# Transposed inputs and GpSimd-queued weights in the in-projection of a hybrid attention and gating layer, with early maxima by key block and re-laid attention pools

## The chip, the cores and the metric

The kernel runs on one core of a Trainium2 chip. The metric is the device time of one execution in microseconds, lower is better; before and after are compared on the same chip. Of the core's engines, TensorE (PE) multiplies matrices, VectorE (DVE), ScalarE (ACT) and GpSimd (POOL) work on elements, and SyncE (SP) only issues transfers here.

## The reference

One pre-norm layer on 2048 tokens of width 1024, all in float32: an input projection, eight heads of attention with forget gates beside a spatial gating unit, an output projection, a gated feed-forward, and a last norm. What matters here is the projection and attention.

```python
xn = rms_norm(x, mix_norm_g)                       # x / rms(x) * gain
h = xn @ w_in                                      # widths: q 512, k 512, v 512, f 8, z 1024
log_f = log_sigmoid(f_logit + b_f); c = cumsum(log_f)
s = q @ k.T / 8 + c[:, None] - c[None, :]          # per head, causal
attn = softmax(s) @ v
sgu = spatial_gating(gelu(z), ...)
x = x + concat(rms_norm(attn), rms_norm(sgu)) * on_g @ w_out
x = x + (silu(gate) * up) @ w_down                 # [gate, up] = rms_norm(x) * ffn_g @ w_gu
out = rms_norm(x) * fin_g
```

## The kernel before

**Products.** A float32 factor is kept as two halves in the format fp32r, hi = round(a) and lo = a - hi, and a product is three matmuls: hi·hi, hi·lo and lo·hi. `hi_of` (L101) is a cast on ACT, `lo_of` (L106) a subtraction on DVE. `T` takes a tile from a pool; a pool's `bufs` is how many tiles of one name live at a time. The order of each engine's instructions is set by a tile scheduler from the program order and from when tiles come free, so it differs from the order in which the code is written; what must wait waits on semaphores. Nearly all transfers are issued by SP, in the order that the scheduler gave its queue.

**Stage 1, the in-projection,** goes over four chunks of 512 tokens (`for c in range(NCH)`). For a chunk, `x_prep` loads four tiles of 128 tokens (L202), squares and sums them on ACT (L205), takes the power -1/2 on POOL (L148), scales on DVE (L207), transposes on PE against `ident` (L216: 8 of 128x128 a tile) and makes the halves from PSUM with the norm's gain (hi on ACT L220, lo on DVE L221). They are also stored to `XS`, from which z is made later. x_prep is a generator: its steps for chunk c+1 run between the blocks of chunk c. A chunk's blocks of 24 matmuls are: the forget gates' (`pf`, 16 matmuls, L376), q and k (4 head pairs each, L397) and V (4 token tiles, `v_tile`, L343). Accumulators `mm` have four banks. `load_w` brings a weight in four pieces of 128 x 2 x 512 (512 KB) through `rawp`, two buffers (L163), and makes its halves (L101, L106).

**The gates' rows.** `forget_rows(j)` turns chunk j's gate logits into running sums and writes them to `AUG`, two rows a chunk that are added to the scores as two more rows of the contraction; it writes eight rows of 128 at a time (40 transfers in all), and `load_const` fills the rest of AUG from a row of constants.

**Early maxima.** Softmax needs each query's maximum, and for chunk j the heads 0 to `HE[j]` get theirs in stage 1, during chunk j+1: `early_max` loads the head's queries `A` and key chunks `D` (four buffers), and `row_max` runs, for each of four query tiles and each key chunk, one matmul (L275) and one reduction on DVE (L277, on the diagonal L280). `max_split` and `max_rows` (L293, L295) turn the result into a row. `between(n)` runs n of these evaluations in the slot behind each block, n = 3, 6, 6 in chunks 1, 2, 3 (from `EB = 12`), and steps the other generators.

**Stage 2, attention,** frees stage 1's pools and opens its own. For each key block `qk` makes scores (L494, L495, on the diagonal a mask L497 from `idr` and `kmask`), exp on ACT (L499) and halves `Ph`, `Pl`; `pv` follows (L510 to L512). V tiles `V0`… carry columns of ones that POOL writes (L445). z's projection (L542) is woven in from `XS` with weights `wzv` and `wzu`, loaded in chunk 3. Output projection and feed-forward follow.

Of the kernel before, what the change touches and what calls it, by code (L numbers as in the profile page):

```python
# [74 lines left out]
def trunk(ctx: ExitStack, tc: tile.TileContext, x, mix_g, w_in, b_f, ln_g, ln_b, w_st, b_st, on_g, w_out,  # L75
# [80 lines left out]
    def load_w(p, src, tag):  # L156

        wh = T(p, [P, KT, 512], F32R, tag + "h")
        wl = T(p, [P, KT, 512], F32R, tag + "l")
        v = src.rearrange("(k p) n -> p k n", p=P)  # L160
        for i in range(4):
            raw = T(rawp, [P, 2, 512], F32, "raw")
            ld(raw, v[:, 2 * i : 2 * i + 2, :])  # L163
# [12 lines left out]
    ld(mixc, mix_g.rearrange("(k p) -> p k", p=P))  # L176
    def load_const():
# [5 lines left out]
        for h in range(H):  # L183
            ldr(AUG[h, 0:8, :].rearrange("r (o n) -> r o n", n=CH),
                CR[4:5].rearrange("r (o n) -> r o n", o=1).broadcast_to([8, NCH, CH]))
            ldr(AUG[h, 8:10, :].rearrange("r (o n) -> r o n", n=CH),
                CR[32:34].rearrange("r (o n) -> r o n", o=1).broadcast_to([2, NCH, CH]))

    CR = T(dram, [34, CH], F32R, "CR")
    wv = None  # L190

    def x_prep(c, xh, xl):
        xp = p1 if c % 2 else xev
        for i in range(4):
            xh.append(T(xp, [P, 2, CH], F32R, "xh", bufs=4))
            xl.append(T(xp, [P, 2, CH], F32R, "xl", bufs=4))
        xts = {}

        def scaled(tt):
            t = c * 4 + tt  # L200
            xt = T(p1x, [P, D], F32, "xt")
            ld(xt, x[t * P : (t + 1) * P, :])  # L202
# [1 line left out]
            ss = T(p1, [P, 1], F32, "ss")
            nc.scalar.activation(jk, xt, AF.Square, accum_out=ss)  # L205
            r = rsqrt(p1, ss, 1.0 / D, "r1")
            nc.vector.tensor_scalar_mul(xt, xt, r)  # L207
            xts[tt] = xt

        def turned(tt):  # L210
            t, xt = c * 4 + tt, xts[tt]
            o = slice(tt * P, (tt + 1) * P)
            for g in range(2):
                tp = T(ps1, [P, 4, P], F32, "tp")
                for kk in range(4):
                    nc.tensor.transpose(tp[:, kk, :], xt[:, (g * 4 + kk) * P : (g * 4 + kk + 1) * P], ident)  # L216
                for kk in range(4):
                    k = g * 4 + kk
                    h_, l_ = xh[k // 2][:, k % 2, o], xl[k // 2][:, k % 2, o]
                    nc.scalar.activation(h_, tp[:, kk, :], AF.Copy, scale=mixc[:, k : k + 1])  # L220
                    nc.vector.scalar_tensor_tensor(l_, tp[:, kk, :], mixc[:, k : k + 1], f(h_), ALU.mult, ALU.subtract)  # L221
# [999 lines left out]
```

## Time and profile before

| what | us |
|---|---|
| median of 3 executions (2527.21 to 2529.3) | 2529.13 |
| profiled execution | 2529.99 |
| its span | 2528.2 |
| PE busy in it | 2450.9 |
| start to chunk 1's first matmul | 102.5 |
| chunks 1 to 3 | 253.9 |
| last projection matmul to first z matmul | 41.5 |

The profile shows one execution: for each engine the time it was busy, tables of windows and of groups of instructions, and timelines, in which a bracket gives the idle time before an instruction and what released it. A line such as L216 is a line of the kernel before. A PE instruction's shown length is that of its way through the array; the next one starts earlier, so that costs are taken from the distance between starts. The granted clock is PE's, as a share of the full one.

### The profile page before, as it was taken

The numbers are of one execution on the slowest core, as the hardware profiler recorded it, in microseconds if no ns is written. First come the engines' busy times: TensorE is split into PE (matmuls) and PEld (weight loads), VectorE is DVE, ScalarE is ACT, GpSimd is POOL, SyncE is SP. The second block draws the span as 40 slices with busy tenths as digits, with TensorE's granted clock in tenths as the row PEclk, the third lists the DMA queues.
The fourth block names the chain that finished last, engine by engine and source line by source line (L and its number), as shares of the span: only waits on it lengthen the run. The fifth ranks groups of instructions, "written<-read, shape, count | busy, mean of one in ns | idle before, by whom it ended". The sixth has DMA issues, their size and how long they took to land. (4 is left out here: it accounts for less than half of the span.)

```text
span 2528.2 us, 31431 instructions
## 1 busy us (share of the span) xinstructions
PE 2450.9 (97%) x10956; PEld 1962.8 (78%) x10956; DVE 1571.9 (62%) x2636; ACT 1071.2 (42%) x1877; POOL 547.2 (22%) x438
## 2 busy tenths in 40 slices
PE   7999979999999998999999999999999999999998
PEld 5777857787777776887788888878888877888876
DVE  5367464555556657446655555685555586596887
ACT  5333116677776676433433233432332342232333
POOL 0000000000000015112223223233232224454441
PEclk9999989999999998999999999999999999999999
DMA  8654556344333325575432222242322235455354
GB/s 265 207 193 154 183 158 161 96 116 111 97 90 93 111 76 151 172 241 172 158 96 79 84 84 78 83 140 84 97 71 84 84 112 190 174 175 187 133 187 151
DMA packets 348806, 339.89 MB, mean 134 GB/s; under 512 B 54444, under 2 KB 273708, under 8 KB 347624
## 3 DMA queue, kind: packets, MB, share of 16 engines
q1 hardware_dynamic: 348648, 337.88, 43.5%
q8 instruction: 87, 1.43, 0.2%
q14 instruction: 71, 0.58, 0.1%
HBM read 221.74 MB, written 116.72 MB: 134 GB/s over the span
## 5 line engine op out<-in xcount | busy, mean ns | idle before, releaser
L101 ACT CAST wh<-raw 128x512 fp32r<-128x512 f32 (+2 forms) x500 | 309.7, 624 | 809.4 <-PE pp L1163 646.1
L106 DVE TENSOR_TENSOR wl<-raw,wh 128x512 fp32r<-128x512 f32 (+2 forms) x500 | 374.6, 758 | 111.8 <-ACT wh L101 111.4
L106 DVE TENSOR_TENSOR Pl<-Pt,Ph 128x512 fp32r<-128x512 f32 (+1 forms) x320 | 200.8, 633 | 201.5 <-ACT Ph L101 191.4
L894 POOL TENSOR_TENSOR raw<-raw 128x512 f32<-128x512 f32 (+1 forms) x124 | 166.0, 1340 | 549.2 <-DMA raw<-in_w_gu_dram 368.0
L499 ACT ACTIVATE Pt<-st 128x512 f32<-128x512 f32 (+1 forms) x320 | 168.4, 532 | 159.6 <-PE st L495 86.9
L542 PE MATMUL z<-wh,xz 128*128 128x512 f32 x512 | 201.4, 403 | 0.0
L101 ACT CAST Ph<-Pt 128x512 fp32r<-128x512 f32 (+1 forms) x320 | 176.2, 556 | 14.4 <-DVE Pl L106 2.5
L894 DVE TENSOR_TENSOR raw<-raw,raw 128x512 f32<-128x512 f32 (+1 forms) x112 | 133.9, 1197 | 73.9 <-POOL raw L894 69.6
L277 DVE TENSOR_REDUCE mx<-mx_ps 128x1 f32<-128x512 f32 x192 | 128.0, 685 | 32.0 <-PE mx_ps L275 31.0
L275 PE MATMUL mx_ps<-D,A 72*128 72x512 f32 (+5 forms) x320 | 123.6, 409 | 13.3 <-DVE mx L277 5.6
L512 PE MATMUL pv<-Pl,V 128*128 128x512 f32 (+1 forms) x320 | 122.1, 382 | 8.1 <-DVE Pl L106 8.0
L510 PE MATMUL pv<-Ph,V 128*128 128x512 f32 (+1 forms) x320 | 122.8, 384 | 2.4 <-DMA V<-VD 2.0
L494 PE MATMUL st<-A,D 74*128 74x512 f32 (+1 forms) x320 | 122.1, 382 | 0.9 <-ACT Pt L499 0.7
L495 PE MATMUL st<-B,C 128*128 128x512 f32 (+1 forms) x320 | 120.2, 376 | 0.0
L511 PE MATMUL pv<-Ph,V 128*64 128x512 f32 (+1 forms) x320 | 117.4, 367 | 0.0
L542 PEld LDWEIGHTS z<-wh,xz 128*128 128x128 f32 x512 | 96.6, 189 | 18.2
L1163 PE MATMUL pp<-R2h,wh 128*128 128x512 f32 x264 | 105.0, 398 | 5.2 <-ACT u L952 5.2
L1163 PE MATMUL pp<-R3h,wl 128*128 128x512 f32 x264 | 104.1, 394 | 2.6 <-DVE wl L106 2.6
L1163 PE MATMUL pp<-R2h,wl 128*128 128x512 f32 x264 | 104.9, 397 | 0.3 <-DVE wl L106 0.2
L1163 PE MATMUL pp<-R1h,wh 128*128 128x512 f32 x264 | 104.4, 395 | 0.3 <-ACT wh L101 0.3
L1163 PE MATMUL pp<-R3h,wh 128*128 128x512 f32 x264 | 104.6, 396 | 0.0
L1163 PE MATMUL pp<-R5h,wh 128*128 128x512 f32 x264 | 104.5, 396 | 0.0
(311 smaller groups left out, 6250.0 us busy)
## 6 DMA issues: line engine op xcount, KB each, us to landing
raw<-in_w_gu_dram SPq DMA_DIRECT2D x88, 512.0 KB
HD<-hT SPq DMA_DIRECT2D x44, 512.0 KB
xz<-XS SPq DMA_DIRECT2D x32, 512.0 KB
XA<-xa SPq DMA_DIRECT2D x27, 512.0 KB
xa<-XA SPq DMA_DIRECT2D x24, 512.0 KB
raw<-HD SPq DMA_DIRECT2D x24, 512.0 KB
xb<-XA SPq DMA_DIRECT2D x24, 512.0 KB
XA<-xb SPq DMA_DIRECT2D x21, 512.0 KB
```

The costliest lines, as they stand in the source:

```text
L101: nc.scalar.copy(o, i)
L106: eng.tensor_tensor(o, i, f(h), ALU.subtract)
L275: nc.tensor.matmul(pm[:, 0:n], lhs, rhs_of(s, n), start=True, stop=True)
L277: nc.vector.tensor_reduce(mx[:, a, s : s + 1], pm, AX.X, ALU.max)
L494: nc.tensor.matmul(st[:, off:], Dt[:, b * P : (b + 1) * P], A[:, off:], start=True, stop=False)
L495: nc.tensor.matmul(st[:, off:], C[:, b * P : (b + 1) * P], B[:, off:], start=False, stop=kb < 4 * j)
L499: nc.scalar.activation(Pt[:, off:], st[:, off:], AF.Exp)
L510: nc.tensor.matmul(pv[:, off:], V[:, 0:P], Ph[:, off:], start=kb == 0, stop=False)
L512: nc.tensor.matmul(pv[:, off:], V[:, 0:P], Pl[:, off:], start=False, stop=kb == 4 * j + 3)
L542: nc.tensor.matmul(pz, xz[:, a, k, :], w[b][:, k, :], start=n == 0, stop=n == 3 * KT - 1)
L894: (nc.vector if e == "v" else nc.gpsimd).tensor_tensor(o, a, b, op)
L1163: nc.tensor.matmul(pm, a[:, k, :], b[:, k, :], start=on is None and k == 0 and e == 0, stop=k == it.kh - 1 and e == 2, skip_group_check=n ...
```

## The change

**Transposed input.** The host passes x also transposed (`x_t`). Class `Chunk` takes the place of x_prep: it loads x_t in four pieces of 512 KB a chunk and makes halves straight from them. The norm's factor depends on the token, which now lies along the free axis: the four factors' columns are transposed by PE into a row on all partitions (`row`, 4 transposes a chunk of a broadcast column) and x_t is multiplied by it (`rb`) on DVE. Natural tiles of x are still loaded for the squares. In chunk 0 the halves are made without the factor, and V, q, k, the gates and z are multiplied by it at eviction.

**Start.** 13 matmuls on a tile of zeros (`still`) stand first on PE. Pieces of x_t and of wv (in five pieces) alternate on SP; V of chunk 0 is accumulated k by k in four banks at a time (`v_open`, `v_part`, `v_close`).

**Weights.** wq, wk, wzv and wzu are issued by GpSimd. wzu's first two pieces are asked for behind chunk 3's first V tile, its halves made behind the loop. The gate weight has 40 columns in place of 128.

**Maxima and AUG.** AUG is laid out [block and head, row, 128], and a chunk's rows are written by one transfer; the constants are two, from tiles that POOL sets. `early_max` goes key chunk by key chunk over the four query tiles (`one_max`), with loads j+1 ahead and five D buffers; EB by chunk gives 3, 6 and 7 evaluations a slot.

**Attention's pools.** V0 and V1 get a pool of their own (`p2v`), with their ones set early by DVE; the pool of Pt, Ph and Pl, and the PSUM pools of scores and pv are set apart and re-ordered; idr and kmask are made in the start. `v` has two buffers.

```diff
-EB = 12
+EB = [1, 12, 12, 10]
+ND = 5
-    AUG = T(dram, [H, 10, S], F32R, "AUG")
+    AUG = T(dram, [NB * H, 10, P], F32R, "AUG")
+    def weight(p, src, tag, pieces=PC, eng=nc.gpsimd):
...
+            wide = tag == "wv" and n_raw[0] % 4 > 1
+            raw[i] = T(p1x, [P, 2, 512], F32, "xt") if wide else T(rawp, [P, 2, 512], F32, "raw")
+            raw[i] = raw[i][:, 0 : o.stop - o.start]
+            eng.dma_start(raw[i], v[:, o, :])
...
+    class Chunk:
...
+        def halves(self, i, ms=(0, 1)):
+            raw = self.raw[i]
+            if self.c:
+                nc.vector.tensor_tensor(raw, raw, self.rb.rearrange("p (o n) -> p o n", o=1).broadcast_to([P, 2, CH]),
+                                        ALU.mult)
+            for m in ms:
...
+                nc.scalar.activation(h_, raw[:, m], AF.Copy, scale=mixc[:, k : k + 1])
+                nc.vector.scalar_tensor_tensor(l_, raw[:, m], mixc[:, k : k + 1], f(h_), ALU.mult, ALU.subtract)
...
+        def square(self, tt, xt):
             jk = T(p1, [P, D], mybir.dt.bfloat16, "jk", bufs=1)
+            nc.scalar.activation(jk, xt, AF.Square, accum_out=self.ss[:, tt : tt + 1])
             if tt == 3:
+                a = T(p1, [P, 4], F32, "r1a")
+                nc.vector.tensor_scalar(a, self.ss, 1.0 / D, EPS, ALU.mult, ALU.add)
+                nc.gpsimd.tensor_tensor(r1[:, self.c * 4 : self.c * 4 + 4], a, mhalf, ALU.pow)
+        def row(self):
+            tp = T(ps1, [P, 4, P], F32, "tp")
+            for tt in range(4):
+                t = self.c * 4 + tt
+                nc.tensor.transpose(tp[:, tt, :], r1[:, t : t + 1].broadcast_to([P, P]), ident)
+            self.rb = T(p1, [P, CH], F32, "rb", bufs=1) if self.c else T(p1, [P, CH], F32, "D", bufs=ND)
+            nc.scalar.copy(self.rb, tp.rearrange("p a t -> p (a t)"))
...
-        for b in range(4 * j + 4):
-            ldr(AUG[:, 2 * j : 2 * j + 2, b * P : (b + 1) * P], augs[8 * b : 8 * b + 8])
+        n = 8 * (4 * j + 4)
+        ldr(AUG[0:n, 2 * j : 2 * j + 2, :], augs[0:n])
...
+    def early_max(j):
+        jobs = [(h, s) for h in range(HE[j]) for s in range(j + 1)]
...
+        PF = j + 1
+        for n in range(PF):
+            get(n)
+        for n, (h, s) in enumerate(jobs):
+            get(n + PF)
...
             for a in range(4):
+                one_max(ps1, p1, a, j, s, As[h][:, a * P : (a + 1) * P], Ds[n], mx)
+                yield
...
+        if xc.c:
+            hi_of(nc.scalar, v[:, :, 0:DH], pmv)
+            lo_of(nc.vector, v[:, :, DH:P], pmv, v[:, :, 0:DH])
+        else:
+            r = r1[:, tt : tt + 1]
+            nc.scalar.activation(v[:, :, 0:DH], pmv, AF.Copy, scale=r)
...
+    still = T(p1, [P, CH], F32R, "D", bufs=ND)
+    nc.vector.memset(f(still), 0.0)
+    pm = T(ps1, [P, CH], F32, "mx_ps")
+    for _ in range(13):
+        nc.tensor.matmul(pm, still[:, 0:P], still, start=True, stop=True)
+    wv, get_v, halves_v = weight(wvp, w_in[:, 1024:1536], "wv", [slice(0, 1), slice(1, 2)] + PC[1:], nc.sync)
...
+    wq = whole(wgt, w_in[:, 0:512], "w")
+    load_mats()
+    pms = [v_open() for _ in range(4)]
+    for k in range(KT):
+        for tt in range(4):
+            v_part(pms[tt], nxt, tt, [k])
+    nxt.row()
+    for tt in range(4):
+        v_close(pms[tt], nxt, tt)
+    wk = whole(wgt, w_in[:, 512:1024], "w")
...
+                if c == 0:
...
+                    nc.vector.tensor_tensor(qs, pm, xc.rb, ALU.mult)
...
+            if c == NCH - 1 and tt == 0:
+                wzu, get_u, halves_u = weight(wgt, w_in[:, 1544:2056], "w")
+                get_u(0)
+                get_u(1)
...
+    for i in range(4):
+        if i > 1:
+            get_u(i)
+        halves_u(i)
...
+    p2v = pool(st2, "p2v", bufs=1)
     p2c = pool(st2, "p2c", bufs=1)
+    p2h = pool(st2, "p2h", bufs=2)
     p2 = pool(st2, "p2", bufs=2)
+    psv = pool(st2, "psv", bufs=2, side="right", space=PSUM)
+    pst = pool(st2, "pst", bufs=2, space=PSUM)
...
+    with tc.high_priority():
+        for v in vt[:2]:
+            nc.vector.memset(f(v[:, :, DH:P]), 1.0)
```

What the scheduler makes of it, engine by engine; the name left of the arrow is written, those on its right are read, and "x4" stands for four such rows in a chain. PE at the program's start, before: `tp` are the transposed x, `mm` an accumulator of V.

```order
L216 MATMUL tp_277<-ident_63,xt_239 128x128 x4
L216 MATMUL tp_290<-ident_63,xt_239 128x128 x4
L343 MATMUL mm_303<-wvh_259,xh_231 128x512
L343 MATMUL mm_303<-wvl_260,xh_231 128x512
L343 MATMUL mm_303<-wvh_259,xl_232 128x512
```

PE at the start, after: L438 are the matmuls on zeros, L418 those of V, `mm` of four numbers the four tiles' accumulators.

```order
L438 MATMUL mx_ps_242<-D_240 128x512 x13
L418 MATMUL mm_353<-wvh_256,xh_231 128x512
L418 MATMUL mm_354<-wvh_256,xh_231 128x512
L418 MATMUL mm_355<-wvh_256,xh_231 128x512
L418 MATMUL mm_356<-wvh_256,xh_231 128x512
L418 MATMUL mm_353<-wvl_257,xh_231 128x512
```

The transposes are gone, and V's first matmuls alternate between four accumulators. ACT ahead of chunk 0's gate, after: L102 on `wh` are the casts of wq and wk, L260 the squares, L428 V's evictions, L490 the eviction of the gate.

```order
L102 CAST wh_330<-raw_336 128x1024
L260 ACTIVATE jk_319,ss_239<-xl_311 128x1024
L260 ACTIVATE jk_321,ss_239<-xl_313 128x1024
L102 CAST wh_330<-raw_340 128x1024
L102 CAST wh_330<-raw_344 128x1024
L428 ACTIVATE xh_460<-mm_353,r_2_64 128x8x64
L428 ACTIVATE xh_464<-mm_354,r_2_64 128x8x64
L428 ACTIVATE xh_468<-mm_355,r_2_64 128x8x64
L272 COPY D_458<-tp_453 128x512
L428 ACTIVATE xh_472<-mm_356,r_2_64 128x8x64
L102 CAST wh_476<-raw_478 128x1024
```

The same place on ACT before: L101 on `v` are V's evictions, L220 the halves of x.

```order
L101 CAST v_328<-mm_303 128x8x64
L220 ACTIVATE xh_237<-tp_355,mixc_226 128x128
L101 CAST wh_533<-raw_535 128x1024
L220 ACTIVATE xh_237<-tp_355,mixc_226 128x128
L101 CAST wh_533<-raw_539 128x1024
```

V's evictions now stand in a group behind all four casts of wq. PE at the hand-over to attention, before: L275 are the last head's maxima, L293 turns them into a row, L494 and L495 are the first scores.

```order
L275 MATMUL mx_ps_3583<-D_3508,A_3505 128x512
L275 MATMUL mx_ps_3586<-D_3511,A_3505 128x512
L275 MATMUL mx_ps_3589<-D_3514,A_3505 128x512
L293 MATMUL tp_3627<-ident_63,mh_3624 8x128
L494 MATMUL st_3743<-A_3709,D_3704 128x512
L495 MATMUL st_3743<-B_3712,C_3701 128x512
L494 MATMUL st_3768<-A_3709,D_3704 128x384
```

PE at the hand-over, after: L418 is the last V block's end, L354 the same turn, L624 to L627 the first scores.

```order
L418 MATMUL mm_3259<-wvh_256,xh_1680 128x512
L418 MATMUL mm_3259<-wvl_257,xh_1680 128x512
L418 MATMUL mm_3259<-wvh_256,xl_1684 128x512
L354 MATMUL tp_3189<-ident_63,mh_3186 8x128
L624 MATMUL st_3389<-A_3355,D_3350 128x512
L625 MATMUL st_3389<-B_3358,C_3347 128x512
L627 MATMUL st_3389<-kmask_68,idr_67 128x128
L624 MATMUL st_3414<-A_3355,D_3350 128x384
```

The maxima have moved ahead of the last V block, and the scores follow it directly.

More of the change, by code (lines that the diff above doesn't have):

```diff
@@ L74, in trunk @@
 @with_exitstack
[L75 removed]
+def trunk(ctx: ExitStack, tc: tile.TileContext, x, x_t, mix_g, w_in, b_f, ln_g, ln_b, w_st, b_st, on_g, w_out,
           ffn_g, w_gu, w_down, fin_g, c_mat, c_row, out):
@@ L154, in trunk @@
     rawp = pool(wstk, "rawp", bufs=2, side="right")
-    def load_w(p, src, tag):
+    PC = [slice(2 * i, 2 * i + 2) for i in range(4)]
+    n_raw = [0]
+    def weight(p, src, tag, pieces=PC, eng=nc.gpsimd):
         wh = T(p, [P, KT, 512], F32R, tag + "h")
@@ L182, in load_const @@
         ldr(CR, crr)
[L183 to L202, printed above, removed]
-            jk = T(p1, [P, D], mybir.dt.bfloat16, "jk", bufs=1)
[L204 to L221, printed above, removed]
-            if tt == 3:
-                for i in range(4):
-                    ldr(XS[c][:, 0, 2 * i : 2 * i + 2, :], xh[i])
-                    ldr(XS[c][:, 1, 2 * i : 2 * i + 2, :], xl[i])
-        for fn, tt in ((scaled, 0), (scaled, 1), (turned, 0), (scaled, 2), (turned, 1), (scaled, 3), (turned, 2),
-                       (turned, 3)):
-            fn(tt)
@@ new lines, in trunk @@
+    nxt = Chunk(0)
+    still = T(p1, [P, CH], F32R, "D", bufs=ND)
[4 more added lines that the diff above has]
+    wv, get_v, halves_v = weight(wvp, w_in[:, 1024:1536], "wv", [slice(0, 1), slice(1, 2)] + PC[1:], nc.sync)
+    for m in range(2):
+        nxt.get(0, (m,))
+        get_v(m)
+    for i in range(1, 4):
+        nxt.get(i)
+        get_v(i + 1)
+    for m in range(2):
+        nxt.halves(0, (m,))
+        halves_v(m)
@@ new lines, in trunk @@
+    for i in range(1, 4):
+        nxt.halves(i)
+        halves_v(i + 1)
+    wfr = T(p1, [P, KT, H], F32, "fT", bufs=1)
+    ld(wfr, w_in[:, 1536:1544].rearrange("(k p) n -> p k n", p=P))
+    bfc = T(p1, [H, 1], F32, "bfc", bufs=1)
+    ld(bfc, b_f.rearrange("(h o) -> h o", o=1))
+    nat = [nxt.natural(tt) for tt in range(4)]
+    for i in range(4):
+        nxt.square(i, nat[i])
+    wf = T(p1, [P, KT, 40], F32R, "wf", bufs=1)
+    nc.vector.memset(f(wf), 0.0)
+    nc.vector.tensor_copy(wf[:, :, 0:8], wfr)
@@ L422, in trunk @@
         early = early_max(c) if c < NCH - 1 else iter(())
+    for i in range(4):
+        if i > 1:
+            get_u(i)
+        halves_u(i)
     st1.close()
@@ L437, in trunk @@
     wst_l = T(p2z, [P, 8, P], F32R, "wstl", bufs=1)
[L438 to L444 removed]
+    vt = [T(p2v if i < 2 else p2c, [P, 4, 192], F32R, f"V{i}", bufs=1) for i in range(NC_)]
+    with tc.high_priority():
+        for v in vt[:2]:
+            nc.vector.memset(f(v[:, :, DH:P]), 1.0)
+    for v in vt[2:]:
         nc.gpsimd.memset(f(v[:, :, DH:P]), 1.0)
@@ L474, in prep @@
             for a in range(4):
-                yield from row_max(ps2, p2, a, j, A[0:72, a * P : (a + 1) * P],
-                                   lambda s, n: kd[h, s][1][0:72, 0:n], mx)
+                for s in range(j + 1):
+                    one_max(ps2, p2, a, j, s, A[0:72, a * P : (a + 1) * P], kd[h, s][1], mx)
+                    yield
             mh = max_split(p2, j, mx)
```

239 lines of the change are left out of this document (145 added, 94 removed).

## The prediction

> **What bounds the kernel now.** I read the page's first and third parts, then a table of windows that I cut where the work changes kind, then the timelines of the two windows in which TensorE (PE) isn't full.
>
> ```profile
> span 2528.2 us, 31431 instructions
> PE 2450.9 (97%) x10956; PEld 1962.8 (78%) x10956; DVE 1571.9 (62%) x2636; ACT 1071.2 (42%) x1877; POOL 547.2 (22%) x438
> q1 hardware_dynamic: 348648, 337.88, 43.5%
> ```
>
> PE is busy for 97% of the span, and all but 2 MB of the 340 MB moved go through one queue, SP's. The columns of the next view are the window and its length, busy time and count of each engine, granted clock, DMA share and GB/s.
>
> ```profile
> 0.00:42.00 42.00, 26.25 (x99) 18.48 (x100) 23.55 (x50) 23.47 (x44) 2.41 (x8) 0.96 0.76 231
> 42.00:102.50 60.50, 59.27 (x271) 46.99 (x269) 26.45 (x63) 25.85 (x58) 2.19 (x4) 1.00 0.65 217
> 102.50:356.40 253.90, 253.21 (x1161) 202.65 (x1160) 153.19 (x467) 69.72 (x145) 5.09 (x10) 1.00 0.56 184
> 356.40:398.00 41.60, 24.08 (x74) 15.71 (x74) 23.35 (x47) 17.14 (x31) 0.88 (x3) 0.63 0.74 194
> 360.00:370.00 10.00, 3.41 (x8) 1.66 (x8) 5.82 (x13) 2.67 (x3) 0.00 (x0) 0.55 0.84 259
> 340.00:350.00 10.00, 10.00 (x46) 7.74 (x45) 8.42 (x21) 0.00 (x0) 0.00 (x0) 1.00 0.17 55
> 8.00:10.00 2.00, 0.00 (x0) 0.00 (x0) 0.49 (x2) 1.74 (x3) 0.56 (x1) 1.00 1.04 406
> ```
>
> The in-projection loses time in its first 42 us, then almost nothing for 300 us (253.2 of 253.9 busy), and then comes a hole of 41.6 us at a clock of 0.63 where it hands over to attention. Behind it, from some 20 attention steps on, the change leaves PE's order as it was. So the gain lies in PE work taken out before 400 us, in the start and in the hole.
>
> **PE work.** The timeline in chunk 0's q and k part (start, duration, line, operands):
>
> ```profile
> 91.30 0.39 PE L397 MATMUL mm<-xh,wh 128*128 128x512 f32 x1
> 91.53 0.60 PE L216 MATMUL tp<-ident,xt 128*128 128x128 f32 x4
> 91.89 0.48 PE L397 MATMUL mm<-xl,wh 128*128 128x512 f32 x1
> 92.20 0.40 PE L397 MATMUL mm<-xh,wl 128*128 128x512 f32 x1
> 92.44 0.40 PE L397 MATMUL mm<-xh,wh 128*128 128x512 f32 x1
> ```
>
> Starts of 512-wide matmuls are 0.233 us apart (91.30 to 91.53). From 91.53 to 92.20 stand four transposes and one matmul: 0.67 - 0.233 = 0.44, so 0.11 us a transpose. All 128 of them go (4 x 4 x 8): 14.1 us. In their place come 4 row transposes a chunk: 16 x 0.11 = 1.8. The 13 dummy matmuls run while PE waits for its first data, and cost nothing as long as that data takes over 13 x 0.43 us (cold spacing below) plus their start, some 7 us; if it came sooner, they would cost the difference, 1 us at most. **Gain 12.3 us**, wherever PE is full or not.
>
> **The start.**
>
> ```profile
> 0.73 1.28 ACT L205 ACT_TABLE_LOAD   x1 [0.73 <-PEq L1210]
> 2.60 1.05 SPq L202 DMA_DIRECT2D xt<-in_x_dram  x2
> 7.65 1.06 ACT L205 ACTIVATE jk<-xt 128x1024 bf16<-128x1024 f32 x1 [5.64 <-DMA xt<-in_x_dram]
> 10.47 1.97 PE L216 MATMUL tp<-ident,xt 128*128 128x128 f32 x8 [10.47 <-DVE r1a L146]
> 15.38 0.63 PE L343 MATMUL mm<-wvh,xh 128*128 128x512 f32 x1
> 15.81 0.57 PE L343 MATMUL mm<-wvl,xh 128*128 128x512 f32 x1
> 16.22 0.40 PE L343 MATMUL mm<-wvh,xl 128*128 128x512 f32 x1
> 102.50 0.50 PE L376 MATMUL mm<-xh,wf 128*128 128x512 f32 x1
> L101 ACT CAST wh<-raw 128x1024 fp32r<-128x1024 f32 x16 | 16.8, 1047 | 45.5 <-DMA raw<-in_w_in_dram 45.5
> L106 DVE TENSOR_TENSOR wl<-raw,wh 128x1024 fp32r<-128x1024 f32 x16 | 19.4, 1223 | 16.9 <-ACT wh L101 16.9
> L277 DVE TENSOR_REDUCE mx<-mx_ps 128x1 f32<-128x512 f32 x72 | 48.9, 686 | 13.8 <-PE mx_ps L275 13.0
> L101 ACT CAST v<-mm 128x512 fp32r<-128x512 f32 x16 | 9.4, 586 | 50.7 <-DMA VD<-v 38.3 <-PE mm L343 6.6 <-PE mx_ps L275 4.4
> ```
>
> Chunk 0 holds 96 V, 16 gate and 192 q and k matmuls: 304 x 0.2325 = 70.7 us. By 102.5, where chunk 1's gate begins, PE has also made 62 x-transposes (chunk 0's 32 and 30 of chunk 1's, 6.8) and some 1 us of gate transposes: 78.5. So the start loses 102.5 - 78.5 = 24.0. Before, the chain to the first matmul is x (landed 7.65, issued 2.6), square, power, scale, transposes, halves. After, it is a quarter-megabyte of x_t, issued first of all, and a scaled copy. Landing time: x needed 5 us from issue for two of 512 KB; my estimate for half of that, issued near 1.2, is 5 to 6. Then x's and wv's first halves on ACT (0.59 each, from the 0.586 row): first V matmul at 7.7, already at the warm spacing. V is made a k-slice at a time for four tiles, 12 matmuls = 2.8 us a slice; ACT needs 0.59 + 0.52 and DVE 0.69 (as the 512-wide L277 takes) + 0.61 for it, and a slice is 0.5 MB, 1.3 us at the 406 GB/s shown, so PE is the slow one: V ends near 30.1 to 30.5. The gate takes a V accumulator, so it waits for a V eviction, which on ACT is queued behind wq's last two casts and needs POOL's power of the norm, which is queued behind the issues of wq on GpSimd. I put the gate at 32.5 to 34.8. With 16 + 192 matmuls (48.4), 8 row transposes (0.9) and 1 of gate transposes the chunk ends at 83 to 85, I take 84.5: loss 84.5 - 72.6 = 12. **Gain 12 us** (14 if evictions don't wait; 4 by the first rival). Chunk 0's four extra DVE scalings a weight (8 x 0.69) hide: DVE is busy 26 of 60 us there. The 8 MB of x_t are 20 us of DMA at 406 GB/s, spread over 340 us of shares of 0.56 to 0.65: nothing. Moved off SP: 16 weight issues, and per chunk 40 writes of the gate rows become 4 in all; SP was not what PE waited for in the middle, so nothing there.
>
> **The middle.** It loses nothing now, so it can only lose. Early maxima come faster: 6 and 7 a slot in chunks 2 and 3 (6 before). A slot is 24 matmuls and 7 maxima, about 7.2 us of PE; DVE has 7 maxima of 0.69, an eviction (0.69), and a share of the x halves, 6.0 to 6.7. The 340:350 row shows that PE stays full with DVE at 84%; at 90% some slots will stall. Bounds 0 and 6 (one 0.69 wait in each of 8 slots of chunk 3): **loss 2 us**, nearer to the row that shows none.
>
> **The hand-over.**
>
> ```profile
> 356.21 0.40 PE L343 MATMUL mm<-wvh,xl 128*128 128x512 f32 x1
> 360.38 0.27 PE L293 MATMUL tp<-ident,mh 128*8 128x128 f32 x1 [3.77 <-DVE mh L106]
> 365.50 0.90 PE L275 MATMUL mx_ps<-D,A 66*128 66x512 f32 x2 [4.44 <-DMA D<-KH]
> 376.42 0.78 PE L494 MATMUL st<-A,D 74*128 74x512 f32 x1
> 380.82 0.69 PE L497 MATMUL st<-kmask,idr 128*128 128x128 f32 x2 [2.56 <-DVE kmask L441]
> 386.80 0.77 PE L510 MATMUL pv<-Ph,V 128*128 128x512 f32 x1 [2.01 <-DMA V<-VD]
> 397.87 0.45 PE L542 MATMUL z<-wh,xz 128*128 128x512 f32 x1
> 379.19 0.58 ACT L101 CAST v<-mm 128x512 fp32r<-128x512 f32 x1 [11.43 <-DMA VD<-v]
> 379.79 1.28 ACT L499 ACT_TABLE_LOAD   x1
> 358.27 1.53 SPq L163 DMA_DIRECT2D raw<-in_w_in_dram  x2
> 361.86 1.04 ACT L101 CAST wh<-raw 128x1024 fp32r<-128x1024 f32 x1 [3.81 <-DMA raw<-in_w_in_dram]
> 357.02 2.36 DVE L106 TENSOR_TENSOR wl<-raw,wh 128x1024 fp32r<-128x1024 f32 x2
> ```
>
> From the last projection matmul to the first z matmul 41.5 us pass. The work in them: the left-over maxima (12 matmuls, 10.5 full widths, 2.45 us), the first attention unit (1280 columns in 5 matmuls each, 12.5 full widths and a mask's 1: 3.1) and the second (7.8): 13.2. So 28.3 are lost. After, the maxima are finished ahead of the last block of V matmuls, the mask and V's ones are made early, keys and V tiles lie in memory that is free before stage 1 ends, and the one v buffer is two. What remains is ACT's chain: eviction 0.58, table 1.28, then exp and cast, 1.2 us a 512-wide key block, as long as PE's five matmuls. That is 3.7 ahead of the first pv and some 3 us of narrow blocks: loss 6 to 7. Bounds: 4 (the chain alone) and 10.7, what lies between 376.42 and 397.87 now (21.5 less 10.8 of work), plus one wait for a load (3.6, from issue 358.27 to cast 361.86): 14. I take 7, nearest to the chain, since each of the waits shown has its cause moved. **Gain 21.3 us.** Late next is z: wzu's last two pieces are fetched when buffers come free, and their halves are made behind everything of stage 1; some 14 us of attention cover them.
>
> The clock makes this hole dearer: 0.55 in 360:370, behind two gaps of 3.8 and 4.4 us. The Trainium skill (TensorE: Matmul & The Clock Gate, Part 1) says that PE's clock is halved after an idle window of about 3.4 us; the trace agrees (0.55 behind gaps of 3.77 and 4.44). By that rule a remaining gap of that length would bring the slow clock back for the attention steps behind it; the third rival prices that from rows.
>
> **The sum.** 12.3 + 12 - 2 + 21.3 = 43.6. The profiled span of 2528.2 becomes 2484.6; 1.8 lie outside it (the profiled execution took 2529.99), so 2486.4; that execution stands 0.9 over the median of 2529.13, so 2485.5: I say 2486. With all terms at their bad ends 12.3 + 4 - 6 + 14.3 = 24.6 (2504.5), at their good ends 12.3 + 14 - 0 + 24.3 = 50.6 (2478.5).
>
> **Rivals.**
> First, slow weights. No row shows a transfer issued by GpSimd: q1 has all. wq's four pieces go two at a time through two buffers, and its last casts stand ahead of V's evictions. From below: like SP's, 3.6 us from issue to cast, nothing lost (a piece could even come sooner, since SP's queue is shorter: a gain under 1). From above: each hop also waits out a pair of DVE instructions (2.36): two hops for wq and up to two more for wk, 5 to 10 us: 2491 to 2496. For it: DVE is dense in the first 25 us. Against: wq has 20 us before it is needed. Chance 0.16. The Trainium skill (SBUF — State Buffer, the trap "DVE blocks DMA" and Who interferes with whom) speaks against this part: transfers issued from GpSimd have their descriptors written by it, which DVE can lock out, and it gives 0.62 us alone and 3.1 beside a DVE copy. By its figures each hop would cost an estimated 2.5 us more, four hops 10, and the sum 2496; no row here shows it.
>
> Second, DVE stalls. The maxima in key-block order put four evaluations on a chain that PE follows, and DVE falls behind in chunks 2 and 3: all of the 6 us, and gate rows late too: 2490 to 2493. For it: DVE 8.42 of 10. Against: five D buffers and loads four ahead. Chance 0.08.
>
> Third, the hole stays half open: the first exp or the first z waits for a load as now, with a slow clock. Loss 14 to 20 in place of 7: 2493 to 2499. For it: each of the waits there had another one right behind it. Chance 0.12.
>
> Fourth, slower than before: GpSimd's weights are starved so that PE waits for wk. It must eat 43.6 us: with four hops for eight pieces, 11 us more each over the 3.6 shown. From 11 on it decides; at 14 it would be 2541. Against: the longest pair of DVE instructions of this kind is the 2.36 above. Chance 0.03. That the change doesn't act (no gain, as the tile scheduler restores the old order) has 0.01: the order shows the transposes gone.
>
> **How the numbers follow.** The forecast has 0.60: 2479 to 2491. The rivals reach to 2499, and the bad ends together to 2504. The range 2474 to 2503 leaves out under 2 in 10: the fourth rival, half of the worst combinations, and a start or hand-over better than my chain (5 us under the forecast's good end). Faster by over 0.2% (about what a measurement of this kernel can tell) has 0.95, within 0.2% 0.02, slower 0.03.
>
> **What would show it.** No x-transposes, and PE's first V matmul at 7 to 8.5 us at a spacing of 0.233; chunk 1's gate matmul near 84.5; from there to the last V matmul some 252 us (253.9, less 66 transposes, plus 8, plus the 2.45 of maxima moved in, plus 2 of stalls); the first z matmul 18 us behind that (10.8 of work and 7 of loss), near 354, with a clock over 0.9. Wrong, if GpSimd's transfers take over 6 us each, if PE's idle time before V's eviction or the gate passes 5 us, or if the first exp waits for a DMA.

## The result, and the profile after

The changed kernel took 2508.3 us (median of 4 runs, 2506.8 to 2512.6) against 2529.2 before: ratio 0.9919, interval 0.9902 to 0.9936. It is faster by 20.9 us, half of the 43.6 forecast, and 5 us outside the range. The profiled execution (2512.6) is the longest of the four.

From the page of the changed kernel, its span, engines and first DMA queue (packets, MB, share):

```profile
span 2510.8 us, 31035 instructions
PE 2437.3 (97%) x10857; PEld 1949.1 (78%) x10857; DVE 1562.2 (62%) x2537; ACT 1054.5 (42%) x1787; POOL 555.6 (22%) x442
q0 software_dynamic: 2304, 8.39, 1.1%
```

The DMA view of the changed kernel's first 100 us, with the group of weight issues on GpSimd (count, KB each, median us from issue to landing):

```profile
DMA packets 17237, 31.32 MB, mean 313 GB/s; under 512 B 3248, under 2 KB 7664, under 8 KB 17232
raw<-in_w_in_dram POOLq DMA_DIRECT2D x10, 512.0 KB, 6.5
```

The same view of the kernel before:

```profile
DMA packets 14814, 22.21 MB, mean 222 GB/s; under 512 B 2978, under 2 KB 7234, under 8 KB 14808
```

GpSimd's transfers have a queue of their own (q0, 8.39 MB), and a piece of 512 KB takes 6.5 us from issue to landing. In the first 100 us 9 MB more are moved than before.

Windows of the changed kernel, with the columns of the prediction's table (V of chunk 0; 32.12 to 48.60, which holds the wait for the gate; 60.30 to chunk 1's gate; chunks 1 and 2; chunk 3; the hand-over). From 48.60 to 60.30 PE has no wait:

```profile
7.57:32.12 24.55, 22.43 (x97) 17.84 (x97) 13.06 (x20) 14.59 (x21) 5.02 (x6) 1.00 0.91 319
32.12:48.60 16.48, 10.17 (x39) 6.37 (x40) 6.64 (x8) 6.95 (x9) 2.21 (x3) 0.79 0.95 317
60.30:101.10 40.80, 31.63 (x134) 25.66 (x134) 20.32 (x35) 12.83 (x21) 1.04 (x1) 0.87 0.89 329
101.10:268.73 167.63, 164.38 (x730) 128.09 (x728) 97.87 (x280) 42.66 (x70) 2.17 (x2) 0.99 0.64 206
268.73:360.44 91.71, 88.91 (x384) 69.11 (x383) 63.97 (x157) 18.92 (x26) 5.27 (x9) 0.98 0.58 172
360.44:377.30 16.86, 11.86 (x50) 8.93 (x48) 7.35 (x13) 11.81 (x22) 0.00 (x0) 0.80 0.87 240
```

PE's timeline at the places the forecast named:

```profile
7.57 1.20 PE L418 MATMUL mm<-wvh,xh 128*128 128x512 f32 x4 [1.21 <-ACT wvh L102]
39.08 0.65 PE L482 MATMUL mm<-xh,wf 128*40 128x512 f32 x1 [6.31 <-DVE xh L429]
69.49 0.47 PE L311 MATMUL tp<-ident,v 128*128 128x128 f32 x1 [9.17 <-DVE v L308]
101.10 0.39 PE L482 MATMUL mm<-xh,wf 128*40 128x512 f32 x1
360.21 0.39 PE L418 MATMUL mm<-wvh,xl 128*128 128x512 f32 x1
377.30 0.45 PE L672 MATMUL z<-wh,xz 128*128 128x512 f32 x1
```

The first V matmul comes at 7.57 (forecast 7.7) and the hand-over takes 17.1 us (forecast 18, before 41.5). But chunk 0's gate comes at 39.08 (32.5 to 34.8), behind V's evictions; PE waits 9.17 for the gates' rows; chunk 1's gate comes at 101.1 (84.5); and from there to the last V matmul it is 259.1 us (252). Two of the signs of being wrong that the prediction named have come: GpSimd's pieces take over 6 us (6.5), and PE's wait before the gate passes 5 (6.31). The clock at the hand-over is 0.80, where over 0.9 was forecast.

Below, **loss** at a time means the time less the PE work issued until then, counted as in the prediction (0.2325 us for 512 columns, 0.11 for a transpose, dummies nothing); it is worked out from all of PE's rows. At 100 us the loss is 23.7 before and 28.5 after; from 100 to 345 us it grows by 5.7 before and 13.6 after. Loss allows comparison where the scheduler has interleaved blocks differently.

What stands ahead of the gate, on ACT's timeline (start, duration, line, operation, tiles; in brackets the idle time before it and its releaser):

```profile
24.27 1.05 ACT L102 CAST wh<-raw 128x1024 fp32r<-128x1024 f32 x1 [5.71 <-DMA raw<-in_w_in_dram]
25.22 1.05 ACT L260 ACTIVATE jk<-xl 128x1024 bf16<-128x1024 f32 x1
35.97 1.04 ACT L102 CAST wh<-raw 128x1024 fp32r<-128x1024 f32 x1 [2.67 <-DMA raw<-in_w_in_dram]
36.92 1.84 ACT L428 ACTIVATE xh<-mm,r 128x512 fp32r<-128x512 f32 x3
```

and on POOL's:

```profile
17.10 0.90 POOL L181 DMA_DIRECT2D raw<-in_w_in_dram  x1 [16.05 <-DVE wvl L107]
26.43 0.95 POOL L215 MEMSET xl<- 128x1024 f32 x1 [5.58 <-ACT jk L260]
27.33 0.72 POOL L181 DMA_DIRECT2D raw<-in_w_in_dram  x1
31.01 1.05 POOL L264 TENSOR_TENSOR r<-r1a,mhalf 128x4 f32<-128x4 f32 x1
```

and on DVE's, the low halves of wq's first piece:

```profile
25.35 1.23 DVE L107 TENSOR_TENSOR wl<-raw,wh 128x1024 fp32r<-128x1024 f32 x1 [5.53 <-ACT wh L102]
```

ACT takes its instructions in order. The first square stands behind wq's first cast and waits for that piece until 24.27. POOL's constants (L215) go into the buffers of the squared tiles and wait for the squares; wq's third piece is issued behind them at 27.33. They hold it back by 0.8 us at most, since its buffer comes free only when the first piece's halves are made, at 26.58. The fourth piece is cast at 35.97, as soon as it has landed, and only then are V's evictions reached.

From 100 to 345 us nearly all of PE's waits (5.7 of 6.0 us) are for DVE, which takes the maxima (`mx`). The two longest, and the clock behind each:

```profile
147.29 0.38 PE L337 MATMUL mx_ps<-D,A 66*128 66x256 f32 x1 [1.74 <-DVE mx L342]
148.20:151.60 3.40, 3.40 (x9) 2.64 (x8) 1.06 (x4) 0.00 (x0) 0.00 (x0) 0.51 0.87 285
307.97 0.50 PE L337 MATMUL mx_ps<-D,A 66*128 66x512 f32 x1 [2.31 <-DVE mx L339]
308.60:311.90 3.30, 3.30 (x9) 2.54 (x8) 2.61 (x6) 2.36 (x4) 0.00 (x0) 0.50 0.12 43
```

Before the first, DVE is busy without a gap (4.00 us from 144 to 148). Before the second it stands idle (DVE's row, then ACT's):

```profile
307.09 0.23 DVE L302 TENSOR_SCALAR v<-v 128x128 f32<-128x128 f32 x1 [2.80 <-ACT v L301]
304.18 1.05 ACT L102 CAST wh<-raw 128x1024 fp32r<-128x1024 f32 x1 [5.61 <-DMA raw<-in_w_in_dram]
```

DVE's next instruction is a step of the gates' rows (L302), the maximum stands behind it, and the step waits for ACT, which waits for a piece of wzv. It is the start's pattern once more.

### The profile page after: what moved, and what is told of

Its sections match the earlier page's. It is cut to its first block, busy times and chain, and to the rows that moved or that the text cites. A ratio compares the mean times of both kernels' runs of the same rounds, so it can differ in the third digit from the quotient of the medians.

```text
span 2510.8 us, 31035 instructions
## 1 busy us (share of the span) xinstructions
PE 2437.3 (97%) x10857; PEld 1949.1 (78%) x10857; DVE 1562.2 (62%) x2537; ACT 1054.5 (42%) x1787; POOL 555.6 (22%) x442
## 3 DMA queue, kind: packets, MB, share of 16 engines
q0 software_dynamic: 2304, 8.39, 1.1%
## 5 line engine op out<-in xcount | busy, mean ns | idle before, releaser
L102 ACT CAST wh<-raw 128x512 fp32r<-128x512 f32 (+2 forms) x500 | 309.3, 624 | 803.0 <-PE pp L1296 648.3
L102 ACT CAST Ph<-Pt 128x512 fp32r<-128x512 f32 (+1 forms) x320 | 176.2, 556 | 13.5 <-DVE Pl L107 2.4
L642 PE MATMUL pv<-Pl,V 128*128 128x512 f32 (+1 forms) x320 | 121.9, 381 | 11.2 <-DVE Pl L107 11.2
L624 PE MATMUL st<-A,D 74*128 74x512 f32 (+1 forms) x320 | 121.5, 380 | 1.8 <-ACT Pt L629 1.7
L1296 PE MATMUL pp<-R1h,wl 128*128 128x512 f32 x264 | 104.4, 395 | 0.7 <-DVE wl L107 0.7
L1296 PE MATMUL pp<-R2l,wh 128*128 128x512 f32 x264 | 104.5, 396 | 0.0
```

The lines of the kernel that those rows point to most:

```text
L102: nc.scalar.copy(o, i)
L624: nc.tensor.matmul(st[:, off:], Dt[:, b * P : (b + 1) * P], A[:, off:], start=True, stop=False)
L642: nc.tensor.matmul(pv[:, off:], V[:, 0:P], Pl[:, off:], start=False, stop=kb == 4 * j + 3)
L1296: nc.tensor.matmul(pm, a[:, k, :], b[:, k, :], start=on is None and k == 0 and e == 0, stop=k == it.kh - 1 and e == 2, skip_group_check=n ...
```

## Experiments

The medians of the kernel before in these comparisons were 2526.7 to 2529.7.

**Who or what makes the start slow: queue, bytes or order?**

e1, all weights by SP:

```diff
-    def weight(p, src, tag, pieces=PC, eng=nc.gpsimd):
+    def weight(p, src, tag, pieces=PC, eng=nc.sync):
```

> All weights are issued by SP again, nothing else in the code changes (the scheduler then puts two of wq's casts behind V's evictions on ACT, and the forget rows' first transpose 41 matmuls later on PE). Theory Q (GpSimd's queue is what is slow): a weight piece that takes 6.5 us from issue to landing falls to some 4, chunk 0's gate starts at 34 in place of 39.1, chunk 1's gate at 88 to 92 in place of 101.1, time 2494 to 2499. Theory D (the 16 DMA engines are full in the first 100 us, 31.3 MB, whoever issues): pieces stay at 6 to 7 us, and what is gained comes only from the other order on ACT and PE: chunk 1's gate at 94 to 101, time 2500 to 2508.

Measured 2508.0 (ratio 0.9917, 0.9902 to 0.9932), no gain, but the profile is another one: chunk 0's gate at 29.9, chunk 1's at 82.4, loss at 100 us 9.6 in place of 28.5. All that is lost again, 26.7 us from 100 to 345, and in a hand-over of 27 us. Theory Q has the direction of the start right, and the start gains more than its 88 to 92; its time is wrong, and so is its mechanism, since the pieces don't come faster by SP (shown below at e5).

e2, less bytes (`natural` returns tile 0's tile for the other three):

> Of a chunk's four natural tiles of x only the first is loaded, and all four squares are taken from it, so the norms' factors of three tiles in four are another tile's; all instructions of the engines stay, 12 transfers of 512 KB go. Theory D: 3 to 4.5 MB less in the first 100 us, 10 to 14 us of full DMA engines: the power of chunk 0 is ready 5 us sooner, the gates' rows land sooner, PE's idle time of 9.2 us before the rows' transpose falls under 3 and chunk 1's gate comes at 86 to 92: 2494 to 2500. Theory Q: the weights still come at their pace, gate of chunk 0 at 39, stall as before, 2505 to 2510.

Measured 2502.9 (0.9892, 0.9876 to 0.9909). The loss at 100 us is 27.9: the start did not move. That alone is a weak test, since e2 still moves 28.7 MB in these 100 us at a DMA share of 0.84 (0.90 in the changed kernel). The stronger one is e1, which moves 30.3 MB at a share of 0.89 and loses only 9.6. So full DMA engines are not what held the start. The 5 us of e2 came later (loss grows by 5.9 from 100 to 345, in place of 13.6); by what way isn't shown.

e3, chunk 1's x asked for later (`XG = 2` to `XG = 0`), and e4, the gates' rows three slots later in the order:

> Chunk 1's x is asked for one step a slot in chunk 0 in place of three, the bytes stay. Theory D: between 40 and 66 us some 3 MB less are queued ahead of the gates' rows, which land 2 to 3 us after their issue in place of 7; PE's idle time of 9.2 before the rows' transpose falls to 3 to 5 and the row of norms, now 54 PE rows later, isn't waited for; chunk 1's gate at 93 to 96, 2500 to 2504. Theory Q: wk's pieces set the gate's eviction on ACT and so the rows; stall stays at 8 to 9, 2506 to 2510. If the later loads make chunk 1's x late: PE idle before chunk 1's gate, over 2508.

> The forget rows' steps begin three slots later in each of the program's first slots: their first transpose stands 137 PE rows (32 us) later, and the row of norms of chunk 1 comes 16 rows earlier. Theory O (order: PE stands behind one late chain with other work ready): the 9.2 us before the rows' transpose go, chunk 1's gate at 91 to 93, 2497 to 2501. Theory D: the row of norms takes its place, since chunk 1's natural x lands at 63 and its power at 65.5 whatever the order: PE idle 8 to 12 us before the norms' transposes, 2506 to 2512.

e3: 2507.8 (0.9914, 0.9899 to 0.9929), the wait for the gates' rows is still 8.3 us (9.2). e4: 2506.4 (0.9908, 0.9893 to 0.9922): the wait for the gates' rows went, and one of 8.3 us before the norms' transposes took its place, as its second reading said. Neither later loads nor another place of the one chain cures it.

**Which weights.** e5 splits them, e6 splits the other way, e7 gives SP only wq, e8 gives chunk 0's loads and squares the scheduler's highest priority with all weights by GpSimd:

```diff
-    wq = whole(wgt, w_in[:, 0:512], "w")
+    wq = whole(wgt, w_in[:, 0:512], "w", nc.sync)
...
-    wk = whole(wgt, w_in[:, 512:1024], "w")
+    wk = whole(wgt, w_in[:, 512:1024], "w", nc.sync)
```

> wq and wk are issued by SP, wzv and wzu stay with GpSimd. If the start's loss lies in who issues wq and wk, and the loss of chunk 3 and the hand-over with SP (108 and 27 us there, 91.5 and 17 with GpSimd) lies in who issues wzv and wzu, the two halves of gain add: chunk 1's gate at 82 to 84, the first z matmul 275 to 278 us behind it, time 2487 to 2492. If the order that the scheduler gives chunks 1 to 3 follows from the start's and not from z's weights, chunk 3 stays at 100 to 108: 2500 to 2508.

> The reverse: wq and wk by GpSimd, wzv and wzu by SP. By the first reading both losses stand: chunk 1's gate at 100 to 102, chunk 3 and hand-over 10 to 25 us longer than with all by GpSimd, time 2518 to 2533. By the second reading 2506 to 2510.

> Only wq is issued by SP; wk, wzv and wzu by GpSimd. If what costs is that wq's casts stand ahead of the squares and of V's evictions on ACT, with POOL's constants and power between its issues: chunk 0's gate at 30 and chunk 1's gate at 83 to 88, 2488 to 2494. If wk's slow pieces, cast ahead of the gates' eviction, matter as much: chunk 0's gate at 30, but PE waits 5 to 9 us before the gates' transpose, chunk 1's gate at 90 to 96, 2496 to 2503.

> The loads and squares of chunk 0's natural tiles get the scheduler's highest priority, all weights stay with GpSimd: squares stand ahead of wq's casts on ACT, and on POOL the constants and the power ahead of wq's issues, which so wait for the squares. If the order on ACT alone is the cause: the power at 24 in place of 32, chunk 0's gate at 33 to 36 and 2498 to 2504. If it is GpSimd's one queue, in which issues and computing wait for each other: wq is issued from 25 on in place of 17, its third cast, ahead of the evictions, comes at 38 or later, chunk 0's gate at 40 to 46, 2508 to 2515.

| kernel | median, ratio (interval) | loss at 100 us | 100 to 345 |
|---|---|---|---|
| changed | 2508.3, 0.9919 (0.9902 to 0.9936) | 28.5 | 13.6 |
| e5 wq, wk by SP | 2508.6, 0.9912 (0.9893 to 0.9930) | 13.8 | 27.5 |
| e6 wzv, wzu by SP | 2503.8, 0.9897 (0.9882 to 0.9912) | 27.6 | 5.3 |
| e7 wq by SP | 2507.1, 0.9909 (0.9893 to 0.9925) | 17.3 | 23.8 |
| e8 squares first | 2501.6, 0.9890 (0.9875 to 0.9905) | 27.3 | 5.6 |

The gains don't add as I expected of e5: 14.7 us of start are won, and 13.9 given back before 345. Of the start, wq is 11.2 (28.5 to 17.3) and wk 3.5; e7's second reading holds for the start (PE waits 6.9 us for the gates' rows), and not for the time.

e6 missed too; it won where I expected a loss. But its hand-over is 27.4 us, as in e1 and against 17.1 in the changed kernel and 16.7 in e5: with z's weights issued by SP, PE waits 9.6 us for the first exp, which on ACT stands behind V's last eviction and a cast of wzu (PE's waits: in total, times, longest; then ACT's cast):

```profile
PE st L624 <- ACT Pt L629: 9.8, 2, 9.6
359.31 1.04 ACT L102 CAST wh<-raw 128x1024 fp32r<-128x1024 f32 x1 [2.90 <-DMA raw<-in_w_in_dram]
```

So z's weights by GpSimd are worth some 10 us at the hand-over, whoever issues wq and wk.

e8 kept its slow start (27.3; its first V matmul came 4.3 us later, since the natural tiles now load first) and won in the middle. Its chunk 0's gate at 40.0 fits the second reading, its time the first. The power comes at 9.98 there in place of 31.01, and still V's first eviction (37.91) comes right behind wq's third cast and the next (42.24) behind its fourth. So the squares aren't what holds the evictions; wq's casts ahead of them are.

The transfers themselves are hardly slower with GpSimd. In e5, SP's timeline has the issue of wq's first two pieces:

```profile
16.55 3.50 SPq L181 DMA_DIRECT2D raw<-in_w_in_dram  x2
```

and ACT's has their casts, and what stands behind them:

```profile
24.00 1.05 ACT L102 CAST wh<-raw 128x1024 fp32r<-128x1024 f32 x1
25.36 1.06 ACT L102 CAST wh<-raw 128x1024 fp32r<-128x1024 f32 x1 [0.31 <-DMA raw<-in_w_in_dram]
28.35 1.31 ACT L428 ACTIVATE xh<-mm,r 128x512 fp32r<-128x512 f32 x2 [1.93 <-PE mm L418]
34.51 0.58 ACT L490 COPY jk<-mm 8x512 f32<-8x512 f32 x1
```

The first cast comes right behind the squares, so that it doesn't tell when its piece landed. The second waited for its piece, 5.3 us from the end of the issue at 20.05. Of wk's pieces, whose casts in e5 all waited, the shortest took 3.8 us from issue to cast and the longest 7.1; with GpSimd such pieces of wq and wk took 4.9 to 8.8 (17.10 to 24.27 is 7.2). wq's four casts come at nearly the same times: 24.00, 25.36, 32.40 and 33.34 by SP, 24.27, 27.46, 32.26 and 35.97 by GpSimd. What differs is the order on ACT and POOL: here squares stand ahead of wq's casts, V's evictions stand ahead of its last two and wait only for PE (28.35 in place of 36.92), and the gate's eviction stands ahead of wk's casts (34.51 in place of 48.66).

**Where the start's gain went.** e9 gives the early maxima's key loads the highest priority (`with tc.high_priority():` around them) on top of e5; e10 undoes the new order of attention's pools in the changed kernel; e11 has `EB = [1, 12, 12, 12]`, 6 maxima a slot.

> wq and wk by SP, wzv and wzu by GpSimd, and the loads of the early maxima's key tiles get the scheduler's highest priority, so that attention's first loads no longer stand ahead of them; in PE's order the maxima of chunk 3 then stand singly between matmuls, where the kernel with wq and wk by SP has runs of 5 and 6 in a row. Theory B (the start's gain was real, and was lost again in chunk 3 to those runs, in which PE waits for DVE at 0.69 us a maximum and then runs at half clock): the loss that PE piles up from 240 us to the hand-over falls from 21 to under 8, time 2492 to 2498. Theory S (something that doesn't depend on that order holds stage 1's end at 350 to 360, DMA or DVE): 2504 to 2509 again.

> The changed kernel with attention's pools in the order of before (one pool for V, Pt, Ph, Pl; scores and pv in one PSUM pool); mask, v buffers and the early maxima stay. If the pools carry the hand-over's gain: from the last V matmul to the first z matmul 24 to 30 us in place of 17, 2514 to 2521. If the maxima's earlier end, the mask and the v buffers carry it: 17 to 20 us, 2508 to 2512.

> The changed kernel with 6 in place of 7 early maxima a slot in chunk 3. If the loss of chunk 3 (6 us from 300 to 345) is DVE's density there: it falls to 1 to 3, the hand-over may grow by up to 2: 2503 to 2507. If it is the forget rows' and z's weights' chain: no change, 2507 to 2510.

e9: 2513.6 (0.9934, 0.9918 to 0.9951), worse: the runs of maxima are gone, and one wait of another kind has their place (PE's waits):

```profile
PE mx_ps L337 <- DMA KL<-ql: 8.3, 1, 8.3
```

e10: 2502.0 (0.9891, 0.9876 to 0.9905), hand-over 18.5 us: the new order of the pools of V, P and PSUM carries 1.4 us of the hand-over's gain at most. It costs more than that: e10 is 6.3 us faster than the changed kernel, and its loss grows by some 6 us from 100 to 345, in place of 13.6. e11: 2504.3 (0.9899, 0.9884 to 0.9914), the time of its first reading; chunk 3's loss from 300 to 345 fell from 5.7 to 3.3, a little over the 1 to 3 expected.

e12 joins e5, e10 and e11; e13 adds e9; e14 joins e10 and e11; e15 adds e8 to that.

> wq and wk by SP, wzv and wzu by GpSimd, attention's pools as before the change, 6 maxima a slot in chunk 3. If attention's early loads on SP are what gave the start's gain back: the loss between 240 and 345 falls from 21 to under 8 though PE's order still has runs of 4 and 5 maxima, time 2486 to 2492. If the runs do it: loss there 12 to 20, 2496 to 2504.

> The same with the key tiles' loads at the highest priority: no runs of maxima in PE's order, but key tiles are asked for on SP as soon as a buffer is free, ahead of the writes of q and k. If the runs do it: loss between 240 and 345 under 6, 2484 to 2490. If the loads stand in SP's queue ahead of the writes that others wait for, as with the new pools (one wait of 8.3 us): 2495 to 2505.

> The changed kernel, all weights by GpSimd, with attention's pools as before and 6 maxima a slot in chunk 3. The two alone gave 6.3 and 4.0 us. If both take away the same thing (load on chunk 3): 2500 to 2502. If they are two things: 2496 to 2499. The start stays as it is, chunk 1's gate at 100 to 103.

> That, and chunk 0's squares first (6.7 us alone). The cure of the squares lay 1 us in the start and the rest in a chunk 3 that ran without the stall; so together with the other two 2495 to 2500, no sum of the three (which would be 2491).

2506.6 (0.9918, 0.9899 to 0.9938), 2506.1 (0.9914, 0.9891 to 0.9937), 2502.8 (0.9899, 0.9884 to 0.9914) and 2503.1 (0.9901, 0.9884 to 0.9919). All four missed: e14 is no faster than e10 alone, e15 no faster than e8 alone, and e12 and e13 still lose some 19 and 16 us between 240 and 345. e12's expectation rested on an error of mine: the pool of attention's keys stands first in both layouts, so its loads were still early. What they do is seen in e5's timelines, first ACT's:

```profile
233.81 0.56 ACT L102 CAST qh<-mm 128x512 fp32r<-128x512 f32 x1
260.17 0.60 ACT L520 ACTIVATE qh<-mm 128x512 fp32r<-128x512 f32 x1 [8.17 <-issue]
273.18 0.59 ACT L102 CAST v<-mm 128x512 fp32r<-128x512 f32 x1 [5.18 <-DMA VD<-v]
```

SP's (C is a key tile of attention, VD holds V):

```profile
245.44 0.45 SPq L98 DMA_DIRECT2D C<-KH  x1
263.44 0.35 SPq L98 DMA_DIRECT2D KH<-qh  x1
268.21 0.39 SPq L98 DMA_DIRECT2D VD<-v  x1
```

PE's:

```profile
261.55 0.50 PE L509 MATMUL mm<-xh,wh 128*128 128x512 f32 x1 [1.46 <-DVE ql L521]
274.06 0.80 PE L509 MATMUL mm<-xh,wh 128*128 128x512 f32 x1 [1.57 <-DVE ql L521]
```

and the window there (busy PE, PEld, DVE, ACT, POOL; granted clock, DMA share, GB/s):

```profile
270.00:280.00 10.00, 8.24 (x19) 5.53 (x20) 3.64 (x9) 0.59 (x1) 0.00 (x0) 0.50 0.72 230
```

The K half cast at 233.81 is written at 263.44, and behind it the V tile whose halves were done at 233.75 is written at 268.21. Between, SP issues loads of attention and of the maxima, each in its turn. `v` has two buffers, so V's third eviction waits for that write until 273.18. Two V tiles and the gate, whose eviction stands behind theirs on ACT, keep three of the four accumulators; one is left for q, and both of PE's waits end when DVE has evicted the block before (`ql`). The 8.17 us ahead of 260.17 aren't part of it: the block evicted there had only just ended, and e16 has 7.63 in the same place. The clock is slow (0.50) from 270 on.

e16 opens the pool of attention's keys last, so that those loads come behind all writes; e17 is that with 6 maxima.

```diff
-    p2k = pool(st2, "p2k", bufs=3)
     p2v = pool(st2, "p2v", bufs=1)
...
     p2 = pool(st2, "p2", bufs=2)
+    p2k = pool(st2, "p2k", bufs=3)
```

> wq and wk by SP, wzv and wzu by GpSimd as in the kernel that measured 2508.6, and the pool of attention's keys opened last in place of first, so that its loads come behind all writes of Q and K on SP. If those loads ahead of a K write are what gave the start's gain back: no wait of ACT of 8 us in chunk 3, the loss between 240 and 345 falls from 21 to 5 to 8; the hand-over waits for its keys, 2 to 6 us more than 17: 2496 to 2501. If the loss stays at 15 or more, something else holds chunk 3: 2506 to 2512.

> The same with 6 maxima a slot in chunk 3 (4 us alone). By the first reading 2492 to 2498, chunk 3's loss 3 to 6; by the second 2504 to 2509.

2508.4 (0.9931, 0.9909 to 0.9952) and 2509.3 (0.9928, 0.9910 to 0.9945). Both miss the first reading's time. In e16 the loss from 250 to 345 falls from 20.6 (e5) to 9.9, and V's first write goes out at 259.68: that these loads cost some 11 us there is shown. But the hand-over, 32.3 us in place of 16.7, pays it back (PE's waits again):

```profile
PE st L624 <- DMA D<-AUG: 11.5, 1, 11.5
```

The early key loads are thus worth 11 us or more at the hand-over and cost 11 in chunk 3 when the start is fast. e18 keeps them and moves the writes of Q and K to GpSimd's queue, with wq and wk by SP and 6 maxima:

```diff
-                    ldr(QH[pr][c], qh)
-                    ldr(QL[pr][c], ql)
+                    ldw(QH[pr][c], qh)   # nc.gpsimd.dma_start; KH, KL likewise
+                    ldw(QL[pr][c], ql)
```

> wq and wk by SP, wzv and wzu and all writes of Q and K halves by GpSimd, attention's pools as in the change, 6 maxima a slot in chunk 3. If a K write behind attention's loads on SP is the block: loss at 100 us 10 to 14, between 240 and 345 under 8, hand-over as in the changed kernel (16 to 18 us), last pv of attention at 1000 to 1008 in place of 1023.6: 2486 to 2494. If GpSimd's in-order queue blocks in its turn (writes behind weight pieces that wait for a buffer), or key tiles stand behind those loads on SP: 2500 to 2508.

**2493.1 us, ratio 0.9856 (0.9835 to 0.9876)**: 15 us faster than the changed kernel, 35 faster than before. Its windows (first 100 us, to 250, to the last V matmul, the hand-over):

```profile
0.00:100.00 100.00, 89.79 (x376) 69.55 (x377) 52.01 (x81) 46.64 (x68) 14.08 (x27) 0.98 0.94 322
100.00:250.00 150.00, 148.65 (x665) 117.03 (x663) 95.28 (x285) 40.63 (x67) 19.41 (x34) 0.99 0.70 231
250.00:344.40 94.40, 92.03 (x404) 71.19 (x404) 63.80 (x149) 19.38 (x27) 17.94 (x29) 1.00 0.60 182
344.40:358.10 13.70, 9.22 (x46) 6.51 (x44) 6.16 (x11) 11.11 (x22) 0.00 (x0) 1.00 0.80 209
```

Loss at 100 us 16.8 (two waits of 3.7 remain, for the gates' rows and the norms' power), 10.0 from 100 to 345, a hand-over of 13.7 us. No wait at all stands in PE's rows between 250 and 300. The time lies within the first reading; the loss at 100 us is over its 10 to 14. V's writes stay on SP, and here the first three go out at 238.42, 244.58 and 252.50, ahead of attention's keys (256.51). How much of the gain over e5 is the writes' and how much that of 6 maxima was not run apart; in the changed kernel 6 maxima alone gave 4.0 us.

## Why the prediction was wrong, step by step

- **PE work, 12.3:** right as far as the trace shows; no x-transposes are left, and matmuls stand 0.23 apart as before.
- **The start, +12: this step failed.** It came out at -4.5 (from the 24.0 that the prediction counted to 28.5). The chain to V was right (7.57, V done at 30). "I put the gate at 32.5 to 34.8" was not: it came at 39.08. The order that it read was right, evictions behind wq's casts on ACT, but the casts came late: two buffers make wq two hops, and a hop took 4.9 to 7.2 us from issue to cast, against the 3.6 read in the hand-over of before. Second, the wait for the gates' rows (9.2 us; their steps on ACT stand behind casts of wk, and e7 still waits 6.9, e5 0.8) stood in the sum at nothing. With wq and wk by SP, where V's evictions stand ahead of wq's last two casts and the gate's ahead of wk's, the loss at 100 us is 13.8, near the 12 forecast, so e5 shows which term it was. The first rival had the place, with 5 to 10 us; it is 14.7. That the hops are long was right, that GpSimd's queue makes them so was not: by SP they took 3.8 to 7.1, and the order on ACT decides what they cost.
- **That rival's page rule** (the Trainium skill, SBUF — State Buffer, "DVE blocks DMA") has a transfer issued by GpSimd wait for its descriptors while DVE runs an instruction in its two-port mode, such as a float32 copy. Pieces that land in 6.5 us, and take much the same from issue to cast by either queue, give no sign of it. DVE's work beside them was nearly all subtractions and scalings of two tiles, not such copies, so these runs don't put the rule to the test.
- **The middle, -2: this term was too small.** It came out at -9.4 (259.1 us, less transposes and with the maxima moved in, against 253.7). The second rival, DVE stalls with all of the 6 us, is what the trace shows: PE waits 6.0 us from 100 to 345 (1.2 before), and two of the waits bring 3.4 us each at half clock, another 3.4 lost, which no term had. But DVE's density is only a part. Ahead of the longest wait DVE was idle behind the gates' rows and, through ACT, behind a piece of wzv. With 6 maxima a slot (e11) 2.4 us fall away and a wait of 2.5 stays; e6, e8 and e10 lose 5 to 6 and have no wait over 1.0 there. Why the order that e8 and e10 get is free of it isn't settled.
- **The hand-over, +21.3:** right, 41.5 to 17.1 us, 22 with the maxima's 2.45 counted. What carries it is early key loads (e16: 11.5 us of waiting without them) and z's weights by GpSimd (e6 and e1: 27.4 us without), not the new order of V's, P's and PSUM's pools (e10). That the maxima's early end has a part is seen in the order of PE and not shown by a run of its own.
- **x_t's bytes costed at nothing:** the transfers pile up in the first 100 us (31.3 MB against 22.2), not over 340 as I had it; e1 and e5, with 30 MB there and a fast start, show that this is not what held it.
- The sum by first z: 12.3 - 4.5 - 9.4 + 22 = 20.4, measured 397.87 - 377.30 = 20.6. By attention's last pv it is 17.9; behind that point the kernels differ by 0.5, and runs among themselves by up to 8.

## What to carry to other kernels

A transfer that is moved to another engine's queue also changes the order in which a scheduler places what waits for it: read, on every in-order engine, what stands ahead of the instruction that the critical one needs, before costing the transfer itself. A load that is hoisted into free memory is not free: it holds its place in an in-order queue, and a write behind it holds a buffer of the stage that is running. In these runs the hoisted loads and the fast start paid together only once Q's and K's writes had a queue without those loads (e18).
